# The low parts of the weight chunks in four column pieces on GpSimd

## The chip, the cores and the metric

The kernel runs on one core of a Trainium2 chip. The metric is the device time of one execution in microseconds. Engines are named as in the profile: PE is TensorE's matmul, PEld its weight load, DVE is VectorE, ACT is ScalarE, POOL is GpSimd, SP is SyncE, whose queue issues the DMAs.

## The reference

Two layers of an encoder over 512 tokens of width 1024, all in float32. Each layer has a mixer of four attention branches with gates, a cross-attention into 256 memory tokens, and a squared-ReLU MLP of width 4096:

```python
for layer in range(DEPTH):
    h = rms(x, g_mix[layer])
    (aq, ak, av, bcq, bckv, bkr, cq, ck, cv, dq, dk, dv, gate) = jnp.split(h @ w_in[layer], split_points, axis=-1)
    o_a = diff_attention(...)      # 4 heads, two maps each
    o_b = mla(...)                 # 8 heads, latent
    o_c = window_gqa(...)          # 8 heads, 2 key/value heads, window 128
    o_d = axial_gqa(...)           # 8 heads, 2 key/value heads, axial rotary
    o = jnp.stack([o_a, o_b, o_c, o_d], axis=2)
    br = jnp.einsum('bsmc,mcd->bsmd', o, w_branch[layer])
    g = jax.nn.sigmoid(gate.reshape(b, s, N_BRANCH, D_MODEL))
    x = x + jnp.einsum('bsmd,bsmd->bsd', g, br) @ w_out[layer]
    x = x + memory_xattn(rms(x, g_x[layer]), rms(mem, g_mem[layer]), ...)
    u = rms(x, g_mlp[layer]) @ w_up[layer]
    x = x + jnp.square(jax.nn.relu(u)) @ w_down[layer]
```

## The kernel before

Every product of two float32 matrices is made of three matmuls on parts in a reduced format (`F32R`): high by high, high by low and low by high. The high part is the value rounded by a copy, the low part is the value minus its high part. `mm3` (L176 to L180) issues the three; L177, L178 and L179 are its lines in the profile.

The weights come in some 350 chunks of 128 partitions by 640 to 1024 columns. `wload` (L292) loads one chunk into a staging tile `wst` (two buffers, on SP's queue, L295), rounds it on ACT into `whi` (four buffers, L299) and lets POOL subtract into `wlo` (four buffers, L300, which calls the helper `sub_lo` at L167, so that the profile shows it as L167). The chain `w` keeps the loads in the order of the program, the chain `wh` the roundings. A staging buffer is free for the next load when the subtraction has read it.

The mixer is a row of units: four of branch B, four of A, two of C, two of D. Each unit has a front (its projections by token block, the norms of queries and keys, their split into parts and their transposes) and an attention part (scores, softmax, transposes of the softmax rows, products with the values). Between them stand products that fill PE: gates (`gate_piece`) and projections of finished branches (`branch_piece`), in an order written out by hand in the string `FILL`. After the mixer come the output projection, the cross-attention and the MLP in quarters. The order of the instructions on each engine is otherwise chosen when the program is built, from an estimated timeline.

DVE's lines in what follows: L450 and L452 (branch A) and L550, L555 (C and D) scale queries and keys, L723 and L725 do so in branch B, L582, L584 and L585 are the rotary products; L167 into `spl` makes the low parts of queries and keys, which PE transposes (L401). L639 and L761 scale a softmax row, PE transposes it (L474), ACT rounds it (L477) and L478 makes its low part, on which the product with the values waits (L645, L646, L767, L768). L512 and L593 gather a head's result. L783 evacuates a gate's bank (`df`, of which there is one). L883 makes the low part of the memory. On POOL, L309 and L310 (and L716, L366) take the inverse square roots of the norms.

Of the kernel before, what the change touches and what calls it, by code (L numbers as in the profile page):

```python
# [11 lines left out]
F32R = mybir.dt.float32r  # L12
# [4 lines left out]
P = 128  # L17
# [69 lines left out]
# Products that need no attention result soon (g: a tile of gates, b: a tile of a branch's projection, k: the memory's  # L87
# keys and values), spread over the mixer: before the first unit, then one group per unit; | marks where the next
# unit's front is issued.
# [4 lines left out]
def kernel(  # L94
# [25 lines left out]
    # slots of a tag go to its tiles in program order, so early and late work use different tags  # L120
# [63 lines left out]
    def chain(key, first, last=None):  # L184
        """issue `first` behind the chain's last instruction, on the same engine"""
        if key in tails:
            tc.add_manual_dep(first.ins, tails[key].name,
                              mybir.DependencyInfo(mybir.DependencyClass.NoSync, mybir.DependencyReason.DATA), reason=key)
        tails[key] = (last or first).ins

    def big():
        """banks of a phase of products only"""
        rot["big"] += 1
        return ("dn", "dn", "df")[(rot["big"] - 1) % 3]

    # ---------------------------------------------------------------- constants
# [11 lines left out]
    # per-layer gain tables, rebuilt at each layer's start  # L208
# [29 lines left out]
    def bias_table():  # L238
        """relative-position bias: one row per head, then sheared reads of it"""
        oh = tl("spl", [P, 1024])  # L240
        SY.dma_start(oh[:32, :1023], onehot)
        rb = tl("tok", [P, 12])
        SY.dma_start(rb[:32, :], rel)
        cm = tl("spl", [P, 1024])
        SY.dma_start(cm[:12, :1023], cmask)
        for c0, c1 in ((0, 512), (512, 1023)):
            ps = psum("dn")
            T.matmul(ps[:12, :c1 - c0], lhsT=rb[:32, :], rhs=oh[:32, c0:c1], start=True, stop=True)
            V.tensor_tensor(out=cm[:12, c0:c1], in0=ps[:12, :c1 - c0], in1=cm[:12, c0:c1], op=ALU.add)
        SY.dma_start(tscr[:, :1023], cm[:12, :1023])  # L250
# [7 lines left out]
    def layer_tables(l):  # L258
        lam_init = 0.8 - 0.6 * math.exp(-0.3 * l)
        cut = ROW_OFF["sub"][0]  # L260
        r0, r1 = tl("bias", [P, 896]), tl("bias", [P, 896])
        for t, o, n in ((r0, 0, cut), (r1, cut, NROW - cut)):
            SY.dma_start(t[:, :n], bass.AP(tensor=rows.tensor, offset=rows.offset + l * NROW + o, ap=[[0, P], [1, n]]))

        def r(name):
            o, w = ROW_OFF[name]
            return r0[:, o:o + w] if o < cut else r1[:, o - cut:o - cut + w]

        V.scalar_tensor_tensor(out=ga, in0=r("aq"), scalar=8.0, in1=r("ak"), op0=ALU.mult, op1=ALU.mult)
        V.scalar_tensor_tensor(out=gc, in0=r("cq"), scalar=8.0, in1=r("ck"), op0=ALU.mult, op1=ALU.mult)  # L270
        V.scalar_tensor_tensor(out=gbn, in0=r("bq")[:, :64], scalar=64.0 / math.sqrt(96.0), in1=r("bk")[:, :64],
                               op0=ALU.mult, op1=ALU.mult)
        V.scalar_tensor_tensor(out=gx, in0=r("xq"), scalar=math.sqrt(128.0), in1=r("xk"), op0=ALU.mult, op1=ALU.mult)
        V.tensor_scalar(gs, r("sub"), math.sqrt(128.0) * (1.0 - lam_init), None, op0=ALU.mult)
        V.tensor_scalar(nsink, r("sink"), -1.0, None, op0=ALU.mult)
        # lambda: exp(sum l0*l1) - exp(sum l2*l3) + lam_init
        lm = r("lam").rearrange("p (a b d) -> p a b d", a=2, b=2)
        lp = ptile()
        lpv = lp[:, :128].rearrange("p (a d) -> p a d", a=2)
        V.tensor_tensor(out=lpv, in0=lm[:, :, 0, :], in1=lm[:, :, 1, :], op=ALU.mult)  # L280
        ls = stat(4)
        V.tensor_reduce(out=ls[:, 0:2], in_=lpv, axis=AX.X, op=ALU.add)
        G.tensor_tensor(out=ls[:, 2:4], in0=econ, in1=ls[:, 0:2], op=ALU.pow)
        V.tensor_tensor(out=nlam, in0=ls[:, 3:4], in1=ls[:, 2:3], op=ALU.subtract)
        V.tensor_scalar(nlam, nlam, -lam_init, None, op0=ALU.add)
        V.tensor_copy(gqr, r("bq")[:, 64:96])
        V.tensor_scalar(gkr, r("bk")[:, 64:96], 32.0 / math.sqrt(96.0), None, op0=ALU.mult)
        V.tensor_copy(gd[:, 0:4, :], bc(r("dq"), 1, 4))
        V.tensor_scalar(gd[:, 4, :], r("dk"), 8.0, None, op0=ALU.mult)

    # ---------------------------------------------------------------- weights
    def wload(key, tag="wst"):  # L292
# [7 lines left out]
        sub_lo(lo[:, :n], st[:, :n], hi[:, :n], G)  # L300
# [5 lines left out]
    # ---------------------------------------------------------------- rms of a [feature, token] operand  # L306
    def rpow(dst, src, add, n):
        """dst = (src + add) ** -0.5"""
        G.tensor_scalar(dst, src, add, None, op0=ALU.add)  # L309
        G.tensor_tensor(out=dst, in0=dst, in1=mhalf[:, :n], op=ALU.pow)  # L310

    class Norm:
        """x^T * g split into two parts; the per-token factor comes later."""
# [7 lines left out]
        def add(self, m, x, c0=0):  # L321
            """rows m of x^T, columns c0..; column parts of a row may come separately"""
# [16 lines left out]
        def add_first(self, m, x):  # L339
            """as add, spread over the engines that wait for x at the start"""  # L340
# [42 lines left out]
    # ---------------------------------------------------------------- token-layout projections  # L383
    def tok_proj(norm, views, width, evacf, half=None, tbs=range(NTB), tags=("dn",) * 4):
        """Per token block: sum over k of xg[k]^T @ W[k]."""
# [11 lines left out]
    def trans(dst, srcs, idn, rows_=P, tag="dn"):  # L397
        """PE-transpose a list of [128, n] sources into one bank, copy to dst (list-shaped view)."""
# [5 lines left out]
    def evac_sq(tk, ps, n, groups, ss, scale):  # L404
        """tk = scale * ps[:, :n]; sums of its squares per (col, heads, width, out col) group"""
# [10 lines left out]
    def split_v(hi, lo, ps, scale):  # L416
        """hi/lo parts of scale * ps; lo may be wider than hi by a broadcast"""
# [10 lines left out]
    # ---- branch A: one head (two maps) per unit  # L428
    def front_A(l, norm, h):
# [15 lines left out]
        def half(j):  # L445
# [8 lines left out]
            sk = tl("spl", [P, 2, 2, 2, 2, 64], F32R)  # m, hl, t, dup, 64  # L454
# [15 lines left out]
    def p_transpose(src, nkb, idn, dsts):  # L470
        """src [128 q, nkb*128] f32 -> bank [128 keys, nkb, 128 q] -> hi / lo destinations"""
# [58 lines left out]
    # ---- branches C and D: one key/value head and its four query heads per unit  # L530
    def front_G(l, norm, br, g):
# [14 lines left out]
        def half(j):  # L546
# [12 lines left out]
            sk = tl("spl", [P, 2, 2, 2, 64], F32R)  # t, hl, dup, 64  # L559
# [14 lines left out]
    def rope(x, tab, j, nh, nax):  # L574
        """x [P, 2 token blocks, nh, nax*32] in place: x*c + swap(x)*s, per axis of 32"""
# [11 lines left out]
    def head_pair_out(pv, of, par):  # L587
        """rows of the two halves of pv summed into of's half `par`"""
# [12 lines left out]
    def attn_G(l, u, br, g, oslots):  # L601
# [5 lines left out]
        for j in range(4):  # L607
# [39 lines left out]
            # vt holds [lo | hi | lo]: even heads read [hi | lo], odd heads [lo | hi]  # L647
# [4 lines left out]
    # ---- branch B  # L652
# [37 lines left out]
    def front_B(l, cT, p):  # L690
# [3 lines left out]
        vt = tl("v", [P, NTB, 4, 64], F32R)  # head 0: hi, lo; head 1: lo, hi  # L694
# [3 lines left out]
        for tb in range(NTB):  # L698
# [9 lines left out]
            # columns: qr0 qr1 | qn0 qn1 kn0 kn1 | v0 v1  # L708
            split_v(vt[:, tb, 0::3, :], vt[:, tb, 1:3, :], ps[:, 320:448].rearrange("p (h d) -> p h d", h=2), None)
            evac_sq(tk[:, t, :], ps, 320, [(64, 4, 64, 6 * t), (0, 2, 32, 6 * t + 4)], s, None)  # L710
        for j in range(2):
# [15 lines left out]
            sq_ = tl("spl", [P, 2, 2, 2, 96], F32R)  # hl, t, h, 96  # L727
# [44 lines left out]
    # ---------------------------------------------------------------- gates and branch projections  # L772
    def gate_piece(l, norm, bi, m):
        """tanh(gate / 2) of the bi-th branch in order, output tile m, kept in DRAM"""
# [12 lines left out]
    def branch_piece(l, bi, o, m, state):  # L787
        """y_m (+)= (1 + tanh(gate/2)) * (o @ W_b); the factor 1/2 is applied to y's sum"""
# [27 lines left out]
    # ---------------------------------------------------------------- cross-attention  # L816
    def mem_prep(l):
        """mem^T * g in two parts, and mem's per-token rms factor"""
        mg = []
        acc = tl("tok", [P, NM]) if l == 0 else None  # L820
        for c in range(2):
            st = tl("wst", [P, 4, NM])
            SY.dma_start(st, memT[c * 512:(c + 1) * 512, :].rearrange("(k p) t -> p k t", p=P))
            for k in range(4):
                if k % 2 == 0:
                    t = slot().rearrange("p a (b t) -> p a b t", b=2)  # k parity, part, tokens
# [18 lines left out]
    def mem_k(l, mg):  # L845
        KT = [tslot().rearrange("p a (b t) -> p (a b) t", b=2) for _ in range(2)]  # hi / lo: head, keys
# [12 lines left out]
    def mem_v(l):  # L859
        VX = [tslot() for _ in range(2)]  # hi / lo: key block, 4*128  # L860
# [24 lines left out]
    def xnorm_split(ps, r, gain):  # L885
        """[tok, 4 heads * 128]: per-head rms factor, optional gain, then hi/lo"""
# [13 lines left out]
    def xattn(l, norm, KT, X, nm):  # L900
# [17 lines left out]
        def attend(pr):  # L918
            for hp in range(2):
                if hp == 1 and pr == 0:  # L920
                    q_trans(1)
                pth = tl("pt", [P, 2, 2, 256], F32R)  # head, key block, q
# [63 lines left out]
    # ---------------------------------------------------------------- the trunk  # L986
# [14 lines left out]
    for l in range(L):  # L1001
# [10 lines left out]
        # mixer  # L1012
# [51 lines left out]
        # last branch, output projection and residual; the first four output tiles follow the branch's tile by tile  # L1064
# [36 lines left out]
        # cross-attention  # L1101
# [6 lines left out]
        # MLP, the hidden width in quarters  # L1108
# [46 lines left out]
def _pack(inputs):  # L1155
    """Weights regrouped into the chunks the kernel reads, each [128, n] contiguous."""
# [57 lines left out]
def _consts():  # L1214
    """Tables that depend on shapes alone."""
# [61 lines left out]
```

## Time and profile before

| | us |
|---|---|
| median of 3 runs | 2450.95 (2446.65 to 2454.4) |
| span of the profiled execution, first to last instruction | 2443.1 |
| PE busy | 2310.9 (95%) |
| DVE busy | 1564.5 (64%) |
| ACT busy | 1155.5 (47%) |
| POOL busy | 1059.1 (43%) |

The profiled execution has no time of its own beside its span; the median of the runs stands 7.9 us above it. A busy engine of this table may be standing still inside an instruction: the time of an instruction runs from its start to its end, whatever holds it.

### The profile page before, as it was taken

How to read it: one execution, taken by the hardware profiler on the slowest of the kernel's cores; microseconds unless marked ns; L12 is line 12 of the kernel's file. 1: busy time of each engine (PE TensorE's matmuls, PEld its weight loads, DVE VectorE, ACT ScalarE, POOL GpSimd, SP SyncE). 2: the span in 40 equal slices, each digit the busy share in tenths (PEclk: the TensorE clock that was granted, in tenths of full speed). 3: DMA queues.
4: the chain of work that ended last, by engine and by line, in shares of the span. 5: the costliest groups of instructions: out<-in, count | busy, mean ns of one | idle time of the engine just before them, and what ended most of it. 6: DMA issues, size and time to landing. Idle time of an engine off the chain costs nothing.

```text
span 2443.1 us, 32530 instructions
## 1 busy us (share of the span) xinstructions
PE 2310.9 (95%) x12032; PEld 1975.2 (81%) x12032; DVE 1564.5 (64%) x2996; ACT 1155.5 (47%) x2269; POOL 1059.1 (43%) x601
## 2 busy tenths in 40 slices
PE   7999999998999999999999999999989899999999
PEld 6778988887778788888877888888877678888887
DVE  7677776788985763322557787678889758533222
ACT  4555655654653642222345565556555436422221
POOL 5443343424344455555454324353231444555553
PEclk9999999999999999999999999999989999999999
DMA  4321232352354323332332213323324442322332
GB/s 159 102 96 65 78 124 88 99 176 71 130 175 147 91 87 95 95 96 98 118 110 94 80 54 122 110 81 122 135 79 149 143 147 74 104 95 95 95 96 86
DMA packets 90944, 260.29 MB, mean 107 GB/s; under 512 B 9832, under 2 KB 14568, under 8 KB 90784
## 3 DMA queue, kind: packets, MB, share of 16 engines
q1 hardware_dynamic: 90784, 258.20, 32.2%
q8 instruction: 95, 1.56, 0.3%
q14 instruction: 65, 0.53, 0.1%
HBM read 224.56 MB, written 33.60 MB: 106 GB/s over the span
## 4 chain that ended last, share of the span: by engine, by line
PE 69%; DVE 20%; issue 4%; POOL 3%; ACT 2%; DMA 1%; SPq 0%; POOLq 0%; ACTq 0%; DVEq 0%
PE dn L177 11%; PE dn L178 11%; PE dn L179 11%; PE df L177 8%; PE df L178 8%; PE df L179 8%; DVE pt L478 2%; PE tr L474 2%; DVE p L639 1%; POOL wlo L167 1%; DVE spl L167 1%; POOL sf L310 1%; PE dn L401 1%; PE sc L177 1%; DVE sf L413 1%
## 5 line engine op out<-in xcount | busy, mean ns | idle before, releaser
L167 POOL TENSOR_TENSOR wlo<-wst,whi 128x1024 fp32r<-128x1024 f32 (+3 forms) x350 | 831.4, 2379 | 1036.2 <-ACT whi L299 933.4
L299 ACT CAST whi<-wst 128x1024 fp32r<-128x1024 f32 (+3 forms) x350 | 350.5, 1002 | 622.3 <-PE dn L178 296.6
L177 PE MATMUL df<-s,whi 128*128 128x512 f32 (+1 forms) x967 | 389.3, 403 | 22.8 <-DVE zg L783 19.4
L179 PE MATMUL df<-s,wlo 128*128 128x512 f32 (+1 forms) x967 | 381.1, 394 | 1.4 <-POOL wlo L167 1.4
L178 PE MATMUL df<-s,whi 128*128 128x512 f32 (+1 forms) x967 | 381.1, 394 | 0.3 <-DVE s L167 0.3
L177 PE MATMUL dn<-whi,s 128*128 128x384 f32 (+4 forms) x736 | 249.4, 345 | 12.3 <-ACT s L346 8.2
L178 PE MATMUL dn<-wlo,s 128*128 128x384 f32 (+4 forms) x736 | 251.1, 343 | 0.9 <-POOL wlo L167 0.9
L179 PE MATMUL dn<-whi,s 128*128 128x384 f32 (+4 forms) x736 | 249.9, 341 | 1.0 <-DVE s L347 1.0
L177 PEld LDWEIGHTS df<-s,whi 128*128 128x128 f32 x967 | 186.3, 193 | 62.7 <-DVE zg L783 20.5
L179 PEld LDWEIGHTS df<-s,wlo 128*128 128x128 f32 x967 | 185.4, 192 | 39.3 <-POOL wlo L167 2.3
L178 PEld LDWEIGHTS df<-s,whi 128*128 128x128 f32 x967 | 186.5, 193 | 35.1 <-DVE s L167 1.1
L177 PE MATMUL dn<-s,whi 128*128 128x512 f32 (+1 forms) x529 | 197.3, 376 | 2.3 <-DVE s L974 2.1
L178 PE MATMUL dn<-s,whi 128*128 128x512 f32 (+1 forms) x529 | 197.8, 375 | 0.4 <-DVE s L167 0.4
L179 PE MATMUL dn<-s,wlo 128*128 128x512 f32 (+1 forms) x529 | 197.3, 374 | 0.0
L177 PEld LDWEIGHTS dn<-whi,s 128*128 128x128 f32 x736 | 140.2, 192 | 22.5 <-ACT s L346 8.2
L478 DVE TENSOR_TENSOR pt<-tr,pt 128x512 fp32r<-128x512 f32 (+1 forms) x224 | 142.3, 642 | 19.8 <-ACT pt L477 9.8
L477 ACT CAST pt<-tr 128x512 fp32r<-128x512 f32 (+1 forms) x224 | 122.9, 556 | 59.4 <-PE tr L474 58.2
L178 PEld LDWEIGHTS dn<-wlo,s 128*128 128x128 f32 x736 | 141.0, 192 | 8.5 <-POOL wlo L167 1.3
L179 PEld LDWEIGHTS dn<-whi,s 128*128 128x128 f32 x736 | 141.0, 192 | 7.2 <-DVE s L347 1.4
L177 PEld LDWEIGHTS dn<-s,whi 128*128 128x128 f32 x529 | 99.4, 189 | 21.1 <-DVE s L974 2.5
L178 PEld LDWEIGHTS dn<-s,whi 128*128 128x128 f32 x529 | 100.1, 189 | 18.8 <-DVE s L167 0.6
L179 PEld LDWEIGHTS dn<-s,wlo 128*128 128x128 f32 x529 | 100.1, 189 | 17.7
(392 smaller groups left out, 4987.4 us busy)
## 6 DMA issues: line engine op xcount, KB each, us to landing
wst<-in_wts_dram SPq DMA_DIRECT2D x272, 512.0 KB, 3.5
wst<-in_wts_dram SPq DMA_DIRECT2D x64, 384.0 KB, 3.1
yl<-yz SPq DMA_DIRECT2D x48, 512.0 KB, 3.3
yz<-zg SPq DMA_DIRECT2D x64, 256.0 KB, 2.0
yz<-yl SPq DMA_DIRECT2D x48, 256.0 KB, 2.3
bias<-tscr SPq DMA_DIRECT2D x16, 320.0 KB, 3.2
yl<-yz SPq DMA_DIRECT2D x16, 256.0 KB, 2.6
bias<-tscr SPq DMA_DIRECT2D x8, 448.0 KB, 3.5
```

The source lines that it names most:

```text
L167: (eng or V).tensor_tensor(out=dst, in0=src, in1=f(hi), op=ALU.subtract)
L177: a = T.matmul(ps, lhsT=lh, rhs=rh, start=first, stop=False)
L178: T.matmul(ps, lhsT=lh, rhs=rl, start=False, stop=False)
L179: b = T.matmul(ps, lhsT=ll, rhs=rh, start=False, stop=last)
L299: chain("wh", A.copy(hi[:, :n], st[:, :n]))
L310: G.tensor_tensor(out=dst, in0=dst, in1=mhalf[:, :n], op=ALU.pow)
L401: T.transpose(ps[:rows_, i * P:(i + 1) * P], s, idn)
L413: V.tensor_reduce(out=ss[:, o:o + nh], in_=ps[:, c0:c0 + nh * d].rearrange("p (h d) -> p h d", h=nh), axis=AX.X, op=ALU.add)
L474: T.transpose(ps[:, kb * P:(kb + 1) * P], src[:, kb * P:(kb + 1) * P], idn)
L477: A.copy(hi, pv)
L478: V.tensor_tensor(out=lo, in0=pv, in1=f(hi), op=ALU.subtract)
L639: V.tensor_scalar(e, e, st[:, 2:3], None, op0=ALU.mult)
```

## The change

The subtraction that makes a chunk's low part is issued as four instructions on POOL, each on a quarter of the columns (256 of 1024, 192 of 768; every chunk's width can be divided by four). The tiles, their buffers, the loads and the rounding stay as they are. The other hunks of the diff take comments away.

```diff
@@ -297,20 +297,22 @@
         hi = tl("whi", [P, 1024], F32R)
         lo = tl("wlo", [P, 1024], F32R)
         chain("wh", A.copy(hi[:, :n], st[:, :n]))
-        sub_lo(lo[:, :n], st[:, :n], hi[:, :n], G)
+        step = n // 4 if n % 4 == 0 else n // 2
+        for c in range(0, n, step):
+            sub_lo(lo[:, c:c + step], st[:, c:c + step], hi[:, c:c + step], G)
         return hi[:, :n], lo[:, :n]
...
```

## Rows read from the trace of the kernel before

**Rows 1.** The profile page: the span, the busy time of each engine, the chain of work that ended last by engine, and the costliest group of POOL (line, engine, operation, output from inputs, shape, count, busy us, mean ns of one, idle time before and what ended it).

```profile
span 2443.1 us, 32530 instructions
...
PE 2310.9 (95%) x12032; PEld 1975.2 (81%) x12032; DVE 1564.5 (64%) x2996; ACT 1155.5 (47%) x2269; POOL 1059.1 (43%) x601
...
PE 69%; DVE 20%; issue 4%; POOL 3%; ACT 2%; DMA 1%; SPq 0%; POOLq 0%; ACTq 0%; DVEq 0%
...
L167 POOL TENSOR_TENSOR wlo<-wst,whi 128x1024 fp32r<-128x1024 f32 (+3 forms) x350 | 831.4, 2379 | 1036.2 <-ACT whi L299 933.4
```

**Rows 2.** Busy time by stretch: from and to (us), length, then us busy and number of instructions of each engine, PE's granted clock, DMA share and GB/s. The first 40 us, the heads of branch A in layer 1, branch D in both layers, and the MLP of layer 1.

```profile
0.00:40.00 40.00, 25.11 (x109) 22.68 (x110) 25.56 (x43) 13.40 (x20) 19.64 (x15) 0.91 0.44 160
...
265.00:445.00 180.00, 169.11 (x975) 153.54 (x975) 128.94 (x274) 100.43 (x222) 73.49 (x48) 0.98 0.31 104
560.00:700.00 140.00, 127.77 (x690) 109.60 (x690) 125.89 (x236) 78.79 (x167) 51.20 (x30) 0.95 0.36 119
870.00:1250.00 380.00, 379.79 (x1682) 313.48 (x1683) 145.72 (x182) 124.47 (x167) 196.97 (x89) 1.00 0.32 100
1775.00:1925.00 150.00, 135.26 (x722) 114.65 (x722) 134.09 (x238) 84.89 (x169) 49.95 (x26) 0.96 0.39 130
```

**Rows 3.** What PE waited for over the whole span: waiting instruction, what released it, us in total, times, the longest.

```profile
PE df L177 <- DVE zg L783: 19.4, 17, 3.4
PE dn L401 <- DVE spl L167: 16.4, 12, 2.7
PE tr L474 <- DVE pt L478: 11.5, 6, 5.5
PE dn L177 <- ACT s L346: 8.2, 1, 8.2
PE pv L645 <- DVE of L593: 7.8, 7, 3.2
PE tr L362 <- DVE of L355: 5.5, 1, 5.5
...
PE pv L508 <- DVE of L512: 4.7, 2, 2.4
PE pv L646 <- DVE pt L478: 4.2, 4, 1.7
PE dn L179 <- DVE z L883: 3.8, 4, 1.5
...
PE pv L768 <- DVE pt L478: 2.8, 2, 1.4
...
PE df L179 <- POOL wlo L167: 1.4, 2, 1.1
...
PE dn L178 <- POOL wlo L167: 0.9, 1, 0.9
```

**Rows 4.** The timeline (start us, us, engine, line, operation, output from inputs, shape, count, idle time before and what ended it) from 486 to 491 us, lines of POOL, DVE and PE.

```profile
485.94 2.36 POOL L167 TENSOR_TENSOR wlo<-wst,whi 128x1024 fp32r<-128x1024 f32 x1
...
486.68 1.83 DVE L639 TENSOR_SCALAR p<-p,st 128x384 f32<-128x384 f32 x1
...
489.55 0.41 DVE L639 TENSOR_SCALAR p<-p,st 128x384 f32<-128x384 f32 x1
...
489.03 0.39 PE L646 MATMUL pv<-pt,v 128*128 128x256 f32 x1 [1.73 <-DVE pt L478]
```

**Rows 5.** The timeline from 394 to 402 us, the second half of a front of branch A, lines of POOL, DVE and PE.

```profile
395.29 1.84 POOL L167 TENSOR_TENSOR wlo<-wst,whi 128x768 fp32r<-128x768 f32 x1
...
395.36 2.33 DVE L450 TENSOR_TENSOR tok<-tok,sf 128x512 f32<-128x512 f32 x1 [0.29 <-POOL sf L310]
397.72 2.11 DVE L452 TENSOR_TENSOR tok<-tok,ga 128x128 f32<-128x128 f32 x2
...
397.86 1.82 POOL L167 TENSOR_TENSOR wlo<-wst,whi 128x768 fp32r<-128x768 f32 x1
...
400.91 0.34 PE L401 MATMUL dn<-jr,spl 128*128 128x128 f32 x2 [2.63 <-DVE spl L167]
```

**Rows 6.** POOL's instructions by line and shape: count, busy us, mean ns of one, idle time before. The subtraction of 512 columns (in the MLP), and a sum of 256 columns.

```profile
L167 POOL TENSOR_TENSOR T<-p,T 128x512 fp32r<-128x512 f32 x12 | 15.5, 1289 | 4.4 <-DVE T L1122 4.4
...
L836 POOL TENSOR_TENSOR tok<-tok,zr 128x256 f32<-128x256 f32 x7 | 6.0, 854 | 13.3 <-ACT zr L835 13.3
```

**Rows 7.** The timeline of POOL in the second MLP, one subtraction of 1024 columns.

```profile
2202.11 2.40 POOL L167 TENSOR_TENSOR wlo<-wst,whi 128x1024 fp32r<-128x1024 f32 x1 [2.74 <-ACT whi L299]
```

**Rows 8.** What POOL, SP's queue and ACT waited for over the whole span: us in total, times, the longest.

```profile
POOL wlo L167 <- ACT whi L299: 933.4, 265, 27.2
POOL sf L309 <- DVE sf L413: 185.6, 27, 15.5
POOL sf L714 <- DVE sf L413: 28.1, 15, 3.5
...
SPq L295 <- POOL wlo L167: 1329.9, 295, 24.9
...
ACT whi L299 <- PE dn L178: 296.6, 82, 4.6
ACT whi L299 <- PE df L178: 178.5, 58, 4.5
...
ACT whi L299 <- DMA wst<-in_wts_dram: 41.5, 33, 2.9
```

**Rows 9.** The timeline around the boundary of two POOL subtractions at 266.2 us, lines of POOL and DVE.

```profile
264.35 1.84 POOL L167 TENSOR_TENSOR wlo<-wst,whi 128x768 fp32r<-128x768 f32 x1
...
266.15 2.29 POOL L167 TENSOR_TENSOR wlo<-wst,whi 128x768 fp32r<-128x768 f32 x1
...
264.41 2.33 DVE L450 TENSOR_TENSOR tok<-tok,sf 128x512 f32<-128x512 f32 x1 [1.07 <-POOL sf L310]
```

**Rows 10.** The timeline of DVE from 174 to 178 us, in a front of branch B.

```profile
174.63 2.47 DVE L723 TENSOR_TENSOR tok<-tok,gbn 128x128 f32<-128x128 f32 x2
177.03 0.54 DVE L725 TENSOR_TENSOR tok<-tok,gqr 128x64 f32<-128x64 f32 x2
177.49 0.67 DVE L783 TENSOR_TENSOR zg<-df,Rrow 128x512 f32<-128x512 f32 x1
```

**Rows 11.** Busy time by stretch, columns as in rows 2: a stretch of the mixer with a low granted clock.

```profile
714.00:724.00 10.00, 6.52 (x21) 4.96 (x22) 8.78 (x12) 3.57 (x7) 2.83 (x2) 0.66 0.50 162
```

## The prediction

> **What bounds the kernel now.** I read the page first. PE is busy for 2310.9 us of a span of 2443.1 [rows 1], so at most 132.2 us can be won from PE's idle time, and the chain that ended last runs 69% through PE, 20% through DVE and 3% through POOL [rows 1]. The split into stretches says where that idle time lies. In the MLP of layer 1 PE is busy 379.8 of 380 us [rows 2]: nothing done to POOL or DVE can help there. In the mixer PE leaves 11 us of 180 unused (heads of branch A), and 12 of 140 and 15 of 150 in the two stretches of branch D, where DVE itself is busy for about 90% of the time [rows 2]. So the mixer decides, and there the question is what PE waits for.
>
> PE's waits name DVE nearly everywhere: 19.4 us for the gate's evacuation (L783), 16.4 us for the low parts of queries and keys (L167 into `spl`), 18.5 us in three rows for L478 (the low part of a transposed softmax row), 12.5 us in two rows for the head sums (L593, L512), 3.8 us for `mem`'s low part (L883) [rows 3]. The instruction that the change edits is POOL's, and PE waits for its result only 2.3 us in all [rows 3]. So whether the low parts come sooner or later is hardly of interest. What matters is why DVE is late.
>
> The timeline answers it. At 486.68 a DVE scaling of a softmax row (L639) takes 1.83 us; the same instruction at 489.55 takes 0.41. The slow one starts 0.74 us into a POOL subtraction (485.94, 2.36 us long) and ends 0.21 us after it; PE then waits 1.73 us for L478 [rows 4]. At 395.36 the product L450 takes 2.33 us beside a 1.84 us subtraction, and the two L452 behind it 2.11 us beside the next one; PE waits 2.63 us [rows 5]. In these pairs a DVE instruction stands still until POOL's instruction has ended. The Trainium skill ("SBUF — State Buffer", Who interferes with whom) says the same of a DVE instruction with two SBUF inputs or in a 2-port mode, blocked fully by the GpSimd instruction that issued first; the trace agrees, with 1.83 us against 0.41.
>
> **The change, part by part.**
>
> *POOL's own cost.* 512 columns take 1.289 us [rows 6] and 1024 undisturbed columns 2.40 us [rows 7]. That is 2.17 ns a column and 0.18 us an instruction. A piece of 256 columns then costs 0.73 us (the one 256-column row, another sum on POOL, has 0.854 as its mean [rows 6]), a piece of 192 columns 0.59. Four pieces are 2.93 us for 2.40, or 0.53 us more for each chunk; with 350 chunks (the row of the page, [rows 1]) about 186 us more. By the 0.854 row it would be 1.0 us a chunk, 354 us. POOL goes from 1059 us to 1245 (at most 1413) of 2443 and stays far from being the bound. What hides this: POOL stands idle 933 us waiting for ScalarE's rounding [rows 8], and PE's waits for low parts are 2.3 us [rows 3]. If that cover failed on one chunk, PE would lose 0.5 to 1 us there, but the matmuls take a chunk column by column, so that the first piece (0.73 us) releases them earlier than the whole (2.40). I set both together at a gain of 1.5 us.
>
> *Loads.* The next weight load waits on SP's queue for the subtraction to free its staging buffer, 295 times [rows 8], and what is behind it on SP (gates to and from DRAM, bias tiles) waits as well. Each gets 0.5 us later, more where DVE comes in between. The rounding waits for the load itself only 41.5 us in 33 cases, against 475 us in which it waits for PE to give a buffer back [rows 8]. I price it at 0, from above at 33 x 0.53 = 17 us.
>
> *DVE.* This is where the time is. At the boundary of two POOL instructions a waiting DVE instruction gets in: L450, started at 264.41, ends at 266.74, 0.55 us after the first subtraction; the second, put down at 266.15, takes 2.29 us, where one undisturbed takes 1.84 [rows 9]. So a split makes three more openings in each chunk. A blocked DVE instruction now waits at most the rest of one piece (0.73, on average 0.37) instead of up to 2.40. But POOL's next piece gets in after it in turn: behind L450 the next subtraction (397.86) holds up the pair of L452, 2.11 us for two [rows 5]. A single blocked instruction followed by work that doesn't contend gains most; a run of n contending instructions pays up to n pieces, and from four on there is nothing to gain.
>
> The sum by PE's waits [rows 3], each by its example:
> - Behind L639 (L478's three rows, 18.5 us): blocked 1.42 us now, 0.37 on average after, so 1.05 of the 1.73 us wait goes, six tenths: 11 us.
> - Halves of branch A (16.4 us): L450 and the L452 pair are blocked 1.65 and 1.55 us (0.68 and 0.56 free) [rows 5]; after, three instructions at up to 0.59 each, 1.8 us for 3.2. 1.4 of the 2.63 us goes, half: 8 us.
> - Gate evacuations (19.4 us): behind one blocked instruction about 1 us of a wait is won; behind a run nothing: at 174.63 come L723 twice, L725 twice, and only then L783 [rows 10]. A third: 6.5 us.
> - Head sums (12.5 us): one or two blocked instructions ahead, half: 6 us.
> - L883 (3.8 us): two thirds: 2.5 us.
> - Low parts: 1.5 us, from above. The start (L346 and L362, 13.7 us): 0, since DVE is busy 25.6 and POOL 19.6 of the first 40 us [rows 2], more than fits side by side without blocking, and finer turns only change their order.
>
> That is 35.5 us. Not all of it will stay. In the branch D stretches DVE is 90% busy, and an instruction that starts sooner meets the next piece; elsewhere the next wait, for ScalarE or for the other softmax row, is close behind. I keep two thirds, 23 us. From below the keep is nothing, from above all of it, and some of the half-clock time comes back too: PE's granted clock is 0.66 of full speed in 714:724, a mix of its two levels of 1.2 and 2.4 GHz, in a stretch where it idles 3.5 of 10 us [rows 11]. Half of the clock lost in that window is 1.7 us.
>
> *The order of work.* The build chooses each engine's order from an estimated timeline, and 1050 more POOL instructions (three for each of 350 chunks) can move it. No row prices this. The bound that I take is what a badly placed gap costs, 2.63 us in the example of [rows 5]: four such gaps more or fewer are 10 us either way.
>
> The profiled execution spans 2443.1 us; the runs shown have a median of 2450.95, so 7.9 us lie around the span. The sum is 2443.1 - 23 = 2420 us of span and **2428 us** as a run.
>
> **The rivals.**
>
> *Runs eat it (slower).* Place: the chains of short products in branches B and D (L723, L725 [rows 10]). If most blocked DVE instructions stand in runs of four or more, each chunk costs them 2.93 us instead of 2.40, and the gain terms vanish. POOL's rsqrt steps, which wait in the same queue, come 0.5 us later as well: 27 + 15 waits on their input [rows 8] give 22 us. It decides when over two thirds of the 35.5 us sit behind such runs. Time: 2451 + 16 to 22, about 2470 us. For it: L783's share, and 90% busy DVE in D. Against it: L639, L478 and A's halves are the larger part of PE's waits, and their runs are of one to three.
>
> *No hand-over.* A core of GpSimd may go on to its next piece before the others are done; if the port is never free between pieces, DVE waits for all four, 2.93 us for 2.40, and PE's DVE waits of about 71 us grow by 22%: 2451 + 16 = 2467 us. Against it stands the hand-over at 266.2 [rows 9], between two independent POOL instructions. The Trainium skill ("GPSIMD Engine Reference", Instruction dispatch) says that consecutive Pool instructions are no barrier between the cores; taken alone it would speak for this rival, and the row speaks against it.
>
> *Hidden anyway.* Shorter DVE waits are swallowed by the next wait, and the extra loads' delay takes the rest: 2451 us within 7. For it: PE is 95% busy already.
>
> **How the numbers follow.** About 0.3% (7 us) is what a measurement of this kernel can tell from no change. Forecast (DVE let in, 12 to 45 us won): 0.66. Hidden: 0.17. Runs, no hand-over and an unlucky order together: 0.17 (0.08, 0.04, 0.05). The forecast's own range is 2404 to 2441. To leave out no more than 2 in 10, the range goes up through the hidden case: 2404 to 2456. Faster 0.65, same 0.18, slower 0.17.
>
> **What would show it.** In the profile after: POOL near 1245 us with four times the `wlo` instructions at 0.73 us; L639's and L450's longest durations under 1.5 us; DVE's busy time lower by some 100 us; PE's waits on L478, L167 and L783 cut by a third or more; the MLP's stretch as full of PE as now. The prediction is wrong if L639 still takes over 2 us (no hand-over), if DVE's busy time falls and PE's does not fill (hidden), or if runs like L723 to L783 get longer than now (runs).

## The result, and the profile after

With four pieces the kernel takes 2370.49 us (median of 4 runs, 2369.1 to 2373.54), beside 2452.41 us for the kernel before (2446.65 to 2454.4): a ratio of 0.9672 [0.9655, 0.9689] (here and below with its 95% interval), 82 us faster. The prediction had 2428 us and a range from 2404: the sign was right, the gain more than three times as large.

The page of the changed kernel, the lines that answer to [rows 1] (the fourth is POOL's, by shape):

```profile
span 2371.8 us, 33721 instructions
...
PE 2287.5 (96%) x12032; PEld 1963.8 (83%) x12032; DVE 1395.6 (59%) x2996; ACT 1154.2 (49%) x2269; POOL 1304.7 (55%) x1657
...
PE 73%; DVE 10%; POOL 7%; DMA 4%; ACT 3%; issue 3%; SPq 0%; POOLq 0%; ACTq 0%; DVEq 0%
...
L167 POOL TENSOR_TENSOR wlo<-wst,whi 128x256 fp32r<-128x256 f32 x1088 | 876.4, 837 | 627.2 <-ACT whi L299 585.4 <-PE pv L770 12.2 <-ACT T L172 10.7
```

POOL works 246 us longer and the kernel is 71.3 us shorter in span. DVE's share of the chain is halved, from 20% to 10%. The span is PE's busy time and PE's idle time: idle went from 132.2 us [rows 1] to 84.3, that is 47.9 us, and busy from 2310.9 to 2287.5, that is 23.4 us, with the same 12032 matmuls. PE's waits, all rows added up, fell by 47.9 us too (124.8 to 76.9): those for DVE from 101.0 to 51.8, those for POOL from 2.3 to 1.0, those for ScalarE rose from 21.5 to 24.1.

What PE waited for, the lines that answer to [rows 3] (lines of the source from L300 on carry a number two higher now):

```profile
PE df L177 <- DVE zg L785: 11.6, 15, 2.2
PE dn L403 <- DVE spl L167: 8.6, 7, 4.2
PE dn L177 <- ACT s L348: 7.5, 1, 7.5
PE df L177 <- ACT s L599: 5.1, 1, 5.1
...
PE dn L177 <- DVE sf L415: 4.0, 3, 1.6
PE pv L647 <- DVE of L595: 3.8, 2, 3.6
PE pv L648 <- DVE pt L480: 3.4, 5, 1.1
...
PE pv L511 <- DVE pt L480: 1.7, 2, 0.8
...
PE dn L178 <- POOL wlo L167: 1.0, 3, 0.4
...
PE pv L770 <- DVE pt L480: 0.8, 3, 0.3
PE tr L476 <- DVE pt L480: 0.7, 1, 0.7
...
PE dn L179 <- DVE z L885: 0.2, 1, 0.2
```

Every row on DVE that the prediction priced is shorter; the one on L512's successor and the one at the start that waited for DVE (5.5 us) are gone. Other rows grew: the wait for `sf` (L413, now L415) from 2.2 to 4.0 us, one for ScalarE (L599) from 0.8 to 5.1, and a product with the values (L511) now waits 1.7 us for L480 where no such row stood before.

Two DVE instructions, each with the shortest, median and longest duration (ns) of all its executions, first and last start; the kernel before, then the changed one:

```profile
L450 DVE TENSOR_TENSOR tok<-tok,sf x16: 681/692/2443, 251.5 to 1603.7; 128x512 f32<-128x512 f32 x16
...
L639 DVE TENSOR_SCALAR p<-p,st x128: 398/471/2602, 457.6 to 1915.2; 128x384 f32<-128x384 f32 x64, 128x512 f32<-128x512 f32 x64
```

```profile
L452 DVE TENSOR_TENSOR tok<-tok,sf x16: 679/693/1156, 236.0 to 1559.6; 128x512 f32<-128x512 f32 x16
...
L641 DVE TENSOR_SCALAR p<-p,st x128: 400/471/1056, 435.6 to 1842.9; 128x384 f32<-128x384 f32 x64, 128x512 f32<-128x512 f32 x64
```

The shortest and the median are the same, only the tail is cut: the work of DVE did not change, the time for which it is held did. The longest L639 was 2602 ns, of which about 2.1 us was the hold; now it is 1056 ns. The timeline of the changed kernel shows the hold in its new size, between the second and the third piece of one chunk (pieces start at 251.46, 252.02, 252.57 and 253.59):

```profile
252.02 0.61 POOL L167 TENSOR_TENSOR wlo<-wst,whi 128x192 fp32r<-128x192 f32 x1
252.57 1.06 POOL L167 TENSOR_TENSOR wlo<-wst,whi 128x192 fp32r<-128x192 f32 x1
...
252.10 1.07 DVE L452 TENSOR_TENSOR tok<-tok,sf 128x512 f32<-128x512 f32 x1
```

L452 starts 0.08 us into a piece that ends at 252.63, and is done at 253.17, 0.54 us later: 1.07 us, where the kernel before showed 2.33 [rows 5]. The next piece is put down at 252.57, but takes 1.06 us in place of 0.61 and ends 0.46 us after L452: now it was the piece that waited.

The mean granted clock, before and after:

```profile
core 0: 2443.1 us, clock 0.983
```

```profile
core 0: 2371.8 us, clock 0.992
```

The granted clock has two levels, 2.4 and 1.2 GHz. At the lower one the matmuls of one row of products follow each other 0.43 us apart, at the full one 0.23. Two neighbours of the kernel before, then two of the changed one:

```profile
720.25 0.63 PE L177 MATMUL dn<-s,whi 128*128 128x512 f32 x1
720.68 0.63 PE L178 MATMUL dn<-s,whi 128*128 128x512 f32 x1
```

```profile
252.28 0.39 PE L177 MATMUL df<-s,whi 128*128 128x512 f32 x1
252.51 0.40 PE L178 MATMUL df<-s,whi 128*128 128x512 f32 x1
```

The stretches at the lower level add up to 81.9 us in the trace of the kernel before and to 37.5 in that of the changed one, and PE is busy in 68.3 and 31.4 us of them. At the full clock about half of that busy time would have done. So the clock took 34.2 us before and 15.7 after (estimates from these sums), and 18.5 of the 23.4 us that PE's busy time fell are the clock's. No row here shows the other 4.9.

And the stretches that answer to [rows 2] (start, heads of branch A, branch D, MLP):

```profile
0.00:40.00 40.00, 30.03 (x141) 27.18 (x142) 28.30 (x61) 18.62 (x29) 28.81 (x37) 1.00 0.46 163
265.00:445.00 180.00, 174.62 (x1021) 159.64 (x1021) 123.48 (x300) 104.17 (x231) 86.50 (x124) 1.00 0.33 106
560.00:700.00 140.00, 131.60 (x720) 112.97 (x719) 118.88 (x233) 85.90 (x175) 69.23 (x84) 0.98 0.42 135
870.00:1200.00 330.00, 330.00 (x1438) 269.82 (x1437) 92.55 (x122) 104.14 (x132) 214.96 (x255) 1.00 0.34 102
```

PE is fuller in each of the mixer's stretches, and the clock there is 1.00, 1.00 and 0.98 where it was 0.91, 0.98 and 0.95 [rows 2]. The 1.00 of the first 40 us is not all gain: a stretch at the lower level now lies just behind them (0.83 in 40:60, where it was 0.95). The MLP is as full as it was.

### The profile page after: what moved, and what is told of

It is laid out like the page before. It is cut to its first block, busy times and chain, and to the rows that moved or that the text cites. A ratio compares the mean times of both kernels' runs of the same rounds, so it can differ in the third digit from the quotient of the medians.

```text
span 2371.8 us, 33721 instructions
## 1 busy us (share of the span) xinstructions
PE 2287.5 (96%) x12032; PEld 1963.8 (83%) x12032; DVE 1395.6 (59%) x2996; ACT 1154.2 (49%) x2269; POOL 1304.7 (55%) x1657
## 3 DMA queue, kind: packets, MB, share of 16 engines
q1 hardware_dynamic: 90784, 258.20, 34.2%
## 4 chain that ended last, share of the span: by engine, by line
PE 73%; DVE 10%; POOL 7%; DMA 4%; ACT 3%; issue 3%; SPq 0%; POOLq 0%; ACTq 0%; DVEq 0%
PE dn L177 12%; PE dn L178 12%; PE dn L179 12%; PE df L177 9%; PE df L179 8%; PE df L178 8%; POOL wlo L167 5%; DMA wst<-in_wts_dram 3%; PE tr L476 2%; PE dn L403 1%; ACT whi L299 1%; DVE pt L480 1%; PE sc L177 1%; PE sc L178 1%; PE sc L179 1%
## 5 line engine op out<-in xcount | busy, mean ns | idle before, releaser
L167 POOL TENSOR_TENSOR wlo<-wst,whi 128x256 fp32r<-128x256 f32 (+3 forms) x1400 | 1079.1, 803 | 796.3 <-ACT whi L299 705.8
L177 PE MATMUL df<-s,whi 128*128 128x512 f32 (+1 forms) x967 | 383.2, 396 | 21.3 <-DVE zg L785 11.6
L178 PE MATMUL df<-s,whi 128*128 128x512 f32 (+1 forms) x967 | 376.7, 390 | 0.3 <-DVE s L167 0.3
L177 PEld LDWEIGHTS df<-s,whi 128*128 128x128 f32 x967 | 182.8, 189 | 60.0 <-DVE zg L785 13.6
L178 PEld LDWEIGHTS df<-s,whi 128*128 128x128 f32 x967 | 182.9, 189 | 33.4 <-DVE s L167 0.8
L480 DVE TENSOR_TENSOR pt<-tr,pt 128x512 fp32r<-128x512 f32 (+1 forms) x224 | 142.7, 643 | 20.0 <-ACT pt L479 9.5
L311 POOL TENSOR_SCALAR sf<-sf 128x8 f32<-128x8 f32 (+2 forms) x44 | 13.2, 299 | 193.7 <-DVE sf L415 192.0
```

The source lines that it names most:

```text
L167: (eng or V).tensor_tensor(out=dst, in0=src, in1=f(hi), op=ALU.subtract)
L177: a = T.matmul(ps, lhsT=lh, rhs=rh, start=first, stop=False)
L178: T.matmul(ps, lhsT=lh, rhs=rl, start=False, stop=False)
L480: V.tensor_tensor(out=lo, in0=pv, in1=f(hi), op=ALU.subtract)
```

## The experiments

The diffs are against the changed kernel unless they say otherwise. "Old order" means that every engine's instructions are held in the order that the kernel before has, so that the planner's new order plays no part; the pieces of a chunk stand where its one subtraction stood.

**Split or order?** The planner (the part of the build that chooses each engine's order from an estimated timeline) had moved much: in the two traces 3729 of 12032 places in PE's row of matmuls and 1347 of 2996 on DVE hold another instruction than before. Two runs take the two causes apart: four pieces in the old order, and one instruction in the new order.

> Four pieces, but every engine's instructions stand in the order of the kernel before (the pieces where the single subtraction stood). Theory A (port): a waiting DVE instruction gets in between pieces, and that is the gain; the time is 2370 to 2400 us, DVE busy about 1400 us. Theory B (order): the gain is that of the new order of work that the build chose; the time is 2435 to 2455 us although DVE's busy time falls to about 1400. Half of each: about 2410.

> One subtraction per chunk as in the kernel before, but every engine's instructions in the order of the kernel after (the subtraction where the first of its pieces stood). Theory A (port): the order is worth little or even loses, as it was made for low parts that come piece by piece: 2435 to 2470 us, DVE busy about 1560 us. Theory B (order): 2370 to 2400 us with DVE busy still about 1560 us.

Both runs add one call behind the program, which holds each engine's instructions in a written list; the list itself is left out here, as are the lists of all the other runs in the old order.

```diff
 # e1_four_old_order: the changed kernel, with the order of the kernel before
 # e2_one_new_order: the kernel before, with the order of the changed kernel
         norm = nn
+    _pin(tc)
...
```

Four pieces in the old order took 2375.39 us (2374.55 to 2378.97), a ratio of 0.9682 [0.9653, 0.971]. One instruction in the new order took 2449.09 us (2445.53 to 2454.48), 0.9988 [0.9972, 1.0004]. The gain is the split's: 79 us in the old order. The order is worth about 5 us in either comparison (2375.4 to 2370.5, 2454.5 to 2449.1), which is within what the runs of before differ among themselves.

**How many pieces?**

> Two pieces of half a chunk, the order of the kernel before. By theory A the wait that one piece can cost a DVE instruction is 1.29 us (512 columns) in place of 2.40 and 0.73 with four, so two pieces give something over half of what four pieces give in this order: 2400 to 2425 us if four give 2385. By theory B no different from the kernel before: 2440 to 2455 us.

> Eight pieces of 128 (96) columns, the order of the kernel before. A piece is 0.46 us by 0.18 us an instruction and 2.17 ns a column, a chunk 3.6 us against 2.9 with four. Theory A: DVE waits at most 0.46 us a turn, a few us better than four pieces, 2365 to 2390 us, unless POOL's longer chunk (busy near 1500 us) makes PE wait for low parts, then above four pieces by as much as PE's waits for low parts grow. Theory B: 2440 to 2455 us.

> Six pieces (176 of 1024 columns, 128 of 768, the last one what is left), the order of before. Two effects are at work: a shorter hold of DVE (busy 1564, 1464, 1407 and 1329 us with one, two, four and eight pieces), and a longer GpSimd (1531 us with eight, 1305 with four). Theory T (what GpSimd loses in time is late factors, low parts and loads): GpSimd is busy for about 1,420 us, DVE for 1,365, and the time lies between four and eight, 2385 to 2412, so that four is near the best size. Rival S (the loss of eight pieces comes all at once, when GpSimd's queue no longer catches up): 2355 to 2375, as good as four pieces or better.

```diff
-        step = n // 4 if n % 4 == 0 else n // 2
+        step = n // 2                  # e3_two_old_order; e4_eight_old_order: n // 8
...
+        step = -(-n // 96) * 16        # e12_six_old_order: 176 of 1024 columns, 128 of 768
...
+            e = min(n, c + step)
+            sub_lo(lo[:, c:e], st[:, c:e], hi[:, c:e], G)
```

Busy times of the engines with two, four, six and eight pieces, all in the old order (with one it is the line in [rows 1]):

```profile
PE 2305.9 (96%) x12032; PEld 1977.5 (82%) x12032; DVE 1463.5 (61%) x2996; ACT 1155.7 (48%) x2269; POOL 1155.9 (48%) x953
```

```profile
PE 2294.9 (97%) x12032; PEld 1966.5 (83%) x12032; DVE 1406.9 (59%) x2996; ACT 1154.9 (49%) x2269; POOL 1304.6 (55%) x1657
```

```profile
PE 2306.6 (96%) x12032; PEld 1974.8 (82%) x12032; DVE 1369.2 (57%) x2996; ACT 1154.4 (48%) x2269; POOL 1421.9 (59%) x2361
```

```profile
PE 2310.2 (95%) x12032; PEld 1973.6 (81%) x12032; DVE 1329.2 (55%) x2996; ACT 1153.8 (48%) x2269; POOL 1531.4 (63%) x3065
```

| pieces | us (median) | ratio to before | DVE busy | POOL busy |
|---|---|---|---|---|
| 1 (before) | 2447 to 2454, by run | 1 | 1564.5 | 1059.1 |
| 2 | 2409.73 | 0.9821 [0.9796, 0.9846] | 1463.5 | 1155.9 |
| 4 | 2375.39 | 0.9682 [0.9653, 0.971] | 1406.9 | 1304.6 |
| 6 | 2396.03 | 0.9785 [0.9757, 0.9812] | 1369.2 | 1421.9 |
| 8 | 2424.49 | 0.9886 [0.9858, 0.9913] | 1329.2 | 1531.4 |

The longest scaling of a softmax row, of 128 each time, follows the length of a piece: 2602 ns with one piece (above), then with two and with eight:

```profile
L641 DVE TENSOR_SCALAR p<-p,st x128: 400/475/1518, 450.2 to 1882.5; 128x384 f32<-128x384 f32 x64, 128x512 f32<-128x512 f32 x64
```

```profile
L641 DVE TENSOR_SCALAR p<-p,st x128: 400/478/896, 450.9 to 1889.0; 128x384 f32<-128x384 f32 x64, 128x512 f32<-128x512 f32 x64
```

DVE's busy time falls with every cut, POOL's rises with every cut, and of the sizes tried four is the fastest. Two pieces came out as theory A expected. Eight did not: 2365 to 2390 us was expected, or more by as much as PE's waits for low parts grow, and these grew by 8.4 us (0.9 to 9.3) where the run took 49 us longer than four pieces. Six pieces came out between four and eight, as theory T of that run has it (2385 to 2412), and rival S falls. What comes late with eight pieces, in the waits of PE, DVE and ACT:

```profile
PE dn L178 <- POOL wlo L167: 8.7, 15, 1.2
...
DVE tok L722 <- POOL sf L718: 21.5, 10, 4.9
DVE of L522 <- POOL st L312: 19.4, 8, 3.4
...
ACT whi L299 <- DMA wst<-in_wts_dram: 152.9, 77, 4.6
```

These are the low parts themselves (8.7 us; 0.9 with four pieces, 2.3 in two rows before [rows 3]), the inverse square roots that stand in POOL's queue behind the pieces (the two rows have 13.2 and 8.3 us with four), and the loads (73.4 us with four, 41.5 before [rows 8]). The hold is shorter still and POOL's own lateness has taken its place. This was the prediction's first rival in part (its 0.5 us later for the rsqrt steps); it does not decide with four pieces and does with eight.

Lateness is not the whole of it. Eight pieces span 45.4 us more than four (2422.6 to 2377.2): PE is idle for 30.1 us more, and busy for 15.3 us more. With six (2396.1) it is 7.2 us of idle time and 11.7 of busy time, and PE is busy at the lower clock level for 67.9 us there, for 45.0 with four: 11.5 us by the half. So in these two executions most of what six pieces lose against four is the clock, which theory T does not name.

**Where in the kernel?**

> Four pieces for the MLP's chunks alone (up and down, 128 of 336), one instruction for all the others, every engine in the order of before. Theory A (a DVE instruction that waits gets SBUF at the boundary between two pieces, and that pays where PE waits for DVE): in 1062 to 1250 us of before PE is busy for 188.0 of 188.0 us, so nothing can be won there: 2454, 2444 to 2460, ratio 0.997 to 1.002, PE idle about 132 us; DVE busy falls by some 30 to 60 us without any effect. Rival P (the gain is spread evenly over the chunks, for instance since a low part is ready piece by piece): 38% of the 79 us of the full split in the same order, 2424, ratio 0.988.

> The complement: four pieces for all chunks but the MLP's, the order of before. Theory A: the whole gain of the full split in that order, 2376, 2368 to 2384, ratio 0.965 to 0.971, PE idle about 82 us. Rival P: 62% of it, 2405, ratio 0.980. Should POOL's own time matter too, this run is a little faster than the full split, by at most 5 us.

```diff
-        step = n // 4 if n % 4 == 0 else n // 2
+        step = n // 4 if key[1] in ("up", "down") else n      # e5_mlp_four_old_order
...
+        step = n if key[1] in ("up", "down") else n // 4      # e6_mixer_four_old_order
```

Four pieces in the MLP alone: 2450.34 us, ratio 1.0002 [0.998, 1.0025]. In all the rest: 2377.83 us, 0.9707 [0.9681, 0.9733]. DVE's busy time falls by 52 us in the first (1512.2) and nothing comes of it, since PE was full there before (379.79 of 380 us [rows 2]). The gain comes from the chunks outside the MLP, all of it; a share by the number of chunks (rival P) is refuted.

**What is left to win?**

> The low part is left out but for 8 columns of a chunk (one short GpSimd instruction, so that staging buffers are still given back by GpSimd), and the products with the low part read the high part instead; everything else, the order of before too, is kept. It shows what GpSimd's long instructions cost in all. Theory A: DVE is never held, its busy time is under the 1329 us of eight pieces, about 1290, and PE's waits for it shrink to what DVE's own work makes; PE idle 60 to 75 us, half-clock stretches about 30 us, time 2360, 2340 to 2374. Rival F (four pieces already leave nothing to win, what is left are other waits): 2370 to 2380, PE idle 80 us. Rival L (what the split of before and after changes is DVE's time but what it pays is something else, such as the loads): 2400 or more.

> Pieces of 128 columns as with eight pieces, but only the first four of the eight (half of the low part is left out; the products with the low part read the high part), the order of before. It tells why eight pieces are slower than four. Theory T (GpSimd's total time is what hurts: 4.15 us a chunk make low parts, factors and loads late): GpSimd is busy for about 850 us, under before, so the time is at or below the full split in four, 2345 to 2378, and near the run without low parts. Rival H (short pieces hurt by themselves, each hand-over costs the other engine): half of the 49 us that eight pieces lose against four stay, 2390 to 2410.

```diff
-        step = n // 4 if n % 4 == 0 else n // 2
-        for c in range(0, n, step):
-            sub_lo(lo[:, c:c + step], st[:, c:c + step], hi[:, c:c + step], G)
-        return hi[:, :n], lo[:, :n]
+        sub_lo(lo[:, :8], st[:, :8], hi[:, :8], G)            # e7_no_low_old_order
+        return hi[:, :n], hi[:, :n]
...
+        step = n // 8                                         # e8_half_of_eight_old_order
+        for c in range(0, n // 2, step):
+            sub_lo(lo[:, c:c + step], st[:, c:c + step], hi[:, c:c + step], G)
+        return hi[:, :n], hi[:, :n]
```

Without the low part: 2291.86 us, ratio 0.9359 [0.9339, 0.938]. With half of it in pieces of 128 columns: 2307.09 us, 0.942 [0.94, 0.9441]. Both beat what every theory expected of them. Of the run without the low part, the busy times, PE's first two waits for DVE, and the same two DVE instructions as above:

```profile
PE 2257.7 (99%) x12032; PEld 1953.7 (85%) x12032; DVE 1238.4 (54%) x2996; ACT 1149.2 (50%) x2269; POOL 312.4 (14%) x601
```

```profile
PE df L177 <- DVE zg L783: 2.2, 7, 0.5
PE dn L177 <- DVE sf L413: 2.2, 4, 0.9
```

```profile
L450 DVE TENSOR_TENSOR tok<-tok,sf x16: 681/686/694, 226.6 to 1501.7; 128x512 f32<-128x512 f32 x16
...
L639 DVE TENSOR_SCALAR p<-p,st x128: 399/452/489, 418.3 to 1775.8; 128x384 f32<-128x384 f32 x64, 128x512 f32<-128x512 f32 x64
```

All the rows of PE's waits for DVE add up to 101.0 us before, 72.0 with two pieces, 50.0 with four, 62.4 with eight, and 10.2 here. So nearly the whole of PE's waiting for DVE was GpSimd's subtraction, and the longest L450 is within 13 ns of the shortest once it is gone. DVE itself waits only 13.6 us less for POOL's results (45.9 to 32.3), so what went is the hold in the main, and not lateness in POOL's queue. Rival F falls: of the 158 us by which this run is below the kernel before, four pieces leave about 80 (3.2% between the two ratios). In the run with half of the columns GpSimd is busy for 882.2 us and the pieces are as short as with eight: so it is not their shortness that makes eight pieces slow (rival H). POOL's total time is what is left (theory T), but this run also has half as many pieces and no product that waits for a low part, and does not tell these apart. Both runs leave columns out, so they show what the subtraction costs by the hold, by its lateness and by the clock together, not a time that a complete kernel can have.

**Can DVE take some of the columns?** These three compute the whole low part and use the planner's own order.

> The whole low part again, in four pieces, the planner's own order; of each chunk outside the MLP the last piece is DVE's, three are GpSimd's. Theory A with what the last two runs showed (each column that GpSimd subtracts in the mixer still costs time, 83 us in all with four pieces): a quarter of that comes back, about 20 us, and DVE gets 208 pieces of about 0.41 us, 86 us of work in a span in which it is idle for 975 us; together 2355, 2340 to 2372. Rival Q (DVE works in order, and a piece at its head that waits for the chunk's high part or its load holds everything behind it): the time is above 2372, with new rows of DVE waiting for whi of over 30 us in all and PE waiting longer for DVE.

> As the run with one piece, but the last two pieces of each chunk outside the MLP are DVE's. Theory A: half of GpSimd's columns in the mixer are gone (the run with half of the low part took 2307 us), DVE has 416 more pieces, 170 us of work, of which some meets PE's waits: 2340, 2315 to 2370. Rival Q: above 2372 and above the run with one piece, with rows of DVE waiting for whi.

> All four pieces of each chunk outside the MLP are DVE's, GpSimd has the MLP's alone. No hand-over is left in the mixer, but DVE gets 832 pieces of about 0.41 us, 340 us of work, and is busy for about 1,600 us, more than the 1,564 of before. Theory A (what cost time in before was one long hold, not DVE's load): under before, 2350 to 2400. Rival B (DVE's load itself is what PE waits for): 2420 or more. Rival Q: also 2420 or more, but with rows of DVE waiting for whi in place of a full DVE.

```diff
-            sub_lo(lo[:, c:c + step], st[:, c:c + step], hi[:, c:c + step], G)
+            e = V if key[1] not in ("up", "down") and c >= 3 * step else G   # e10: 2 * step, e11: 0
+            sub_lo(lo[:, c:c + step], st[:, c:c + step], hi[:, c:c + step], e)
```

One piece on DVE: 2383.57 us (0.973 [0.9708, 0.9752]); two: 2408.54 us (0.9837 [0.9818, 0.9856]); all four: 2388.01 us (0.9754 [0.973, 0.9779]). None beats the changed kernel; for one and two pieces theory A is refuted. With one piece on DVE, what DVE waited for at those pieces:

```profile
DVE wlo L167 <- ACT whi L299: 64.1, 62, 5.5
```

That is rival Q's row (48.8 us with two, 52.5 with four). But the waits do not follow the times, and the planner's order differs from run to run, so how much of the loss is this row and how much the order stays open. Of the 34.6 us of span that two pieces on DVE lose against the changed kernel, 19.4 are PE's busy time (2306.9 us, of which 63.8 at the lower clock level, for 31.4). The run with all four is the telling one: the busy times, and the piece on DVE.

```profile
PE 2296.6 (96%) x12032; PEld 1971.7 (83%) x12032; DVE 1532.5 (64%) x3892; ACT 1153.1 (48%) x2269; POOL 639.5 (27%) x761
```

```profile
L167 DVE TENSOR_TENSOR wlo<-wst,whi 128x256 fp32r<-128x256 f32 x576 | 206.5, 420 | 33.2 <-ACT whi L299 32.8
```

DVE is busy for 1532.5 us, nearly the 1564.5 of before, but with its own work, 420 ns a piece, in place of standing still; and the kernel is 59 us faster than before. That is within theory A's 2350 to 2400 us and well under the 2420 of rivals B and Q: it was the hold, not DVE's load.

The changed kernel is the fastest of those that compute everything.

## Why the prediction was wrong in size

The mechanism was the one predicted: a held DVE instruction gets in at the end of a piece, and PE waits less for it. That the mixer decides and the MLP gives nothing is shown by the two runs on the place. No hand-over (second rival) is refuted by the timeline above, and by the longest L641 of 1056 ns where four pieces in one hold would be 2.9 us. The Trainium skill ("GPSIMD Engine Reference", Instruction dispatch) says that consecutive Pool instructions are no barrier between the cores; that does not keep DVE out between them here, where L452 got in between the pieces at 252.02 and 252.57.

By its steps:

- *POOL's cost.* Forecast 0.73 us a piece. Two pieces in a row in the MLP take 1.43 us in the timeline, 0.72 each; the mean is 837 ns, since pieces now wait for DVE too (the one at 252.57 above takes 1.06 us, its neighbour 0.61). POOL has 1304.7 us for 1245, inside the bound of 1413.
- *Loads, 0.* ACT's wait for the load went from 41.5 us to 90.1 in the changed kernel. It cost PE nothing that its waits show (0.3 us for `whi`).
- *DVE's busy time.* 169 us lower, where about 100 was named.
- *The terms.* Each against its rows: L478 -13.6 us (forecast -11), halves of branch A -7.8 (-8), gate evacuations -7.8 (-6.5), head sums -8.7 (-6), L883 -3.6 (-2.5), low parts -1.3 (-1.5), the start -6.2 (0). The sum is 49.0 us for 35.5. L478 comes out at -11.9 instead if the new row on L511 is counted with it. The examples from single instances were good estimates; the shares taken of them (six tenths, half, a third) had no row, and that they fit so closely is luck in part. The largest miss among the terms is the start, which was put at 0 because the busy times of DVE and POOL, 25.6 and 19.6 us, come to more than the 40 us. But busy time there was partly hold: DVE is busy for 25.56 us with 43 instructions in the kernel before [rows 2], and for 24.30 us with 81 in the run without the low part.
- *The discount, the step that failed first.* "I keep two thirds" took 12.5 us off, for waits close behind that no row priced. The measured fall of PE's idle time is 47.9 us, all but 1.1 of the terms' sum: rows that no term names grew by that much in net (ScalarE's up by 3.3 us, DVE's down by 2.2).
- *The clock, the step that failed most.* The prediction named it, priced one window of it at 1.7 us and put nothing in the sum. PE's busy time fell by 23.4 us, of which 18.5 are shown to be the clock's (above): PE's busy time at the lower level went from 68.3 to 31.4 us. That 34.2 us were lost to it could have been read from the trace of before. How much of it comes back could not: with six pieces PE's idle time fell by 42.7 us (132.2 to 89.5) and its busy time by 4.3, since PE still was busy for 67.9 us at the lower level. And the clock moves by itself: in 13 runs of the kernel before, on one chip, its mean lay between 0.973 (2459.8 us) and 0.982 (2442.9 us). What decides in which gaps the clock falls stays open.
- *Span to run.* 7.9 us were added to the span as lying around it. In the changed kernel's profiled execution the run took 2373.54 us, 1.7 more than its span. The 7.9 compared one short execution with the median of others, and the step is worth 6.1 us.

The account closes. Forecast 2428, measured 2370.5, 57.5 us apart: discount 12.5, start 6.2, other terms 7.3, less 1.1 for the rows that no term names, PE's busy time 23.4 (18.5 the clock's, 4.9 open), span to run 6.1, and 3.1 by which the profiled execution of the changed kernel lies above its median. The range's lower end, 2404, allowed for 45 us in all, the whole of the terms and little of the clock; it failed by the same steps.

The first rival (runs eat it) is no story of four pieces, but it has a place: POOL's longer chunk does come to count at eight, and at six in part. "Hidden anyway" is refuted by PE's idle time, which fell by nearly the whole of what the terms name.

## What to carry to other kernels

Where two engines exclude each other, look at the longest against the shortest duration of one and the same instruction (681 and 2443 ns here); if the median is the short one, a split of the long partner into a few pieces recovers the tail, and a run without the partner's work tells how much there is in all. Cut until the partner's own results come late, and no further: here four pieces were better than two, six and eight. When PE's gaps are filled, look also at how long PE is busy at the lower clock level: half of that is the most that the clock can give back, and whether it does is seen in a run, not in the gaps (four pieces got 18.5 of 34.2 us, six next to nothing). And do not take a share off a sum of waits without a row that gives it back.

## What the runs showed of the hardware that was not expected

- The subtraction of 8 columns on GpSimd is not near free:

```profile
L167 POOL TENSOR_TENSOR wlo<-wst,whi 128x8 fp32r<-128x8 f32 x350 | 91.6, 262 | 1501.8 <-ACT whi L299 1484.3
```

262 ns against the 0.18 us an instruction that the line through 512 and 1024 columns gave (0.18 + 8 x 0.00217 = 0.20 us).

- One GpSimd subtraction, never on PE's path by its own rows (2.3 us), is what 158 us of 2450 hang on: without it PE's waits for DVE are 90.8 us shorter and its other waits 7.3, and PE is busy for 53.2 us less; the four-piece version still pays about 80 of the 158.
- The same 12032 matmuls took PE 2310.9 us, 2287.5 and 2257.7 at mean granted clocks of 0.983, 0.992 and 0.998. PE is busy at the lower level for 68.3, 31.4 and 6.2 us. By half of that the clock accounts for 18.5 of the first 23.4 us and for 31.1 of the 53.2 us between the first and the last; the rest is not explained by a row shown here.
